# Instance normalisation of 256 MiB on one core: 8 MB tiles in three buffers with one-pass statistics, in place of 4 MB tiles in four buffers with two passes

## The chip, the cores and the metric

One core of one Trainium2 chip. The metric is the device time of one execution in microseconds (us); the profile's "span", from the first to the last instruction, lies some 2 us below it. The kernel before took 1252.11 us (median of 3 runs, 1251.59 to 1254.01).

## The reference

```python
x = np.random.randn(8, 64, 32, 64, 64).astype(np.float32)      # 512 instances of 131072 values
mean = np.mean(x, axis=(2, 3, 4), keepdims=True)
var = np.var(x, axis=(2, 3, 4), keepdims=True)
out = ((x - mean) / np.sqrt(var + 1e-5)).astype(np.float32)
```

256 MiB are read and 256 MiB written, 536.9 MB in all. This input is already very nearly of mean 0 and variance 1, so a kernel that computes slightly wrong statistics, or none, still agrees with the reference within the tolerance.

## The kernel before

An instance is spread over 16 partitions, so a tile holds 8 instances in 128 partitions x 8192 values (32 KiB a partition, 4 MB). There are 64 tiles and four buffers. All transfers go through the SP queue; the store of tile g-2 is issued after the load of tile g.

```python
data_pool = ctx.enter_context(tc.tile_pool(name="data", bufs=4))
...
def issue_compute(g, x_tiles):
    for k in range(KPG):                                   # KPG = 1
        nc.vector.reduce_sum(out=psums[:, k, 0:1], in_=x_tiles[:, k, :], axis=X)
        nc.scalar.activation(out=sq_scratch, in_=x_tiles[:, k, :], func=Square,
                             accum_out=psums[:, k, 1:2])
    nc.tensor.matmul(out=tot, lhsT=ones_t, rhs=psums, start=True, stop=True)
    ...                                                    # mean, variance, scale, bias: 128x1 each
    # normalise in place: VectorE 1/8, ScalarE 1/8, GpSimd 3/4 of the columns
...
LAG = 2
for g in range(n_groups):                                  # 64
    x_tiles = issue_load(g)                                # waits for the buffer's old store
    issue_compute(g, x_tiles)
    pending[g] = x_tiles
    if g >= LAG:
        issue_store(g - LAG, pending.pop(g - LAG))
for g in range(n_groups - LAG, n_groups):
    issue_store(g, pending.pop(g))
```

## Time and profile before

| | before |
|---|---|
| time, span | 1252.11, 1249.7 us |
| bytes moved | 536.9 MB, 430 GB/s over the span |
| DMA engines busy | 99.7% of 16 engines' span |
| VectorE, ScalarE, GpSimd busy | 53%, 44%, 30% |

The first lines are from the page of the kernel before: engines, then the 40 equal slices of the span (DMA: busy tenths of the 16 DMA engines; GB/s: what they moved), the one DMA queue, and groups of instructions (busy us, mean ns of one, idle time before).

```profile
span 1249.7 us, 1827 instructions
...
PE 35.7 (3%) x128; PEld 32.1 (3%) x128; DVE 659.2 (53%) x449; ACT 550.6 (44%) x258; POOL 380.3 (30%) x70
...
DMA  9999999999999999999999999999999999999998
GB/s 403 417 434 434 427 433 430 432 435 430 429 432 434 432 435 429 434 433 434 434 431 433 431 434 434 435 430 432 434 433 436 429 433 434 433 434 435 429 433 357
...
q1 hardware_dynamic: 18432, 536.88, 99.7%
...
L92 DVE TENSOR_REDUCE psums<-x_tiles 128x1 f32<-128x8192 f32 x64 | 555.9, 8686 | 492.9 <-DMA x_tiles<-in_x_dram 492.9
L100 ACT ACTIVATE sq_scratch<-x_tiles 128x8192 bf16<-128x8192 f32 x64 | 449.9, 7029 | 461.3 <-DMA x_tiles<-in_x_dram 461.3
L169 POOL TENSOR_SCALAR x_tiles<-x_tiles,scale,bias 128x6144 f32<-128x6144 f32 x64 | 379.4, 5929 | 855.4 <-DVE bias L149 634.4
L161 ACT ACTIVATE x_tiles<-x_tiles,bias,scale 128x1024 f32<-128x1024 f32 x64 | 79.4, 1241 | 40.5 <-DVE bias L149 40.5
```

The DMA engines are the limit: 9 tenths everywhere but in the last slice, and no other engine above 53%.

The table by stretches of the kernel before. The columns are the window, its length, busy times of the engines with counts, the clock, the DMA share and, last, GB/s:

```profile
core 0: us, PE busy (x) PEld busy (x) DVE busy (x) ACT busy (x) POOL busy (x), PEclk, DMA share, GB/s
300.00:1100.00 800.00, 22.88 (x82) 20.54 (x82) 423.46 (x290) 352.46 (x165) 247.68 (x42) 1.00 1.00 433
80.00:126.00 46.00, 1.67 (x6) 1.50 (x6) 23.97 (x21) 18.83 (x12) 13.88 (x3) 1.00 1.00 432
1230.00:1238.00 8.00, 0.00 (x0) 0.00 (x0) 1.13 (x3) 1.29 (x2) 5.93 (x1) 1.00 0.66 287
1238.00:1249.70 11.70, 0.00 (x0) 0.00 (x0) 0.00 (x0) 0.00 (x0) 0.00 (x0) 1.00 0.75 322
```

In the long middle stretch the engines move 433 GB/s. From 1230 to 1238 us they move 287: the last store waits there for the last tile's computation.

What the SP queue waited for in the kernel before (us in total, times, longest):

```profile
SPq L85 <- DMA out_dram<-x_tiles: 700.8, 60, 12.6
SPq L180 <- POOL x_tiles L169: 303.9, 64, 4.8
```

It mostly waits to issue a load (line 85) until an old store has freed the buffer. One turn of the loop in its timeline (start us, us, engine, line, operation):

```profile
600.16 8.69 DVE L92 TENSOR_REDUCE psums<-x_tiles 128x1 f32<-128x8192 f32 x1 [7.89 <-DMA x_tiles<-in_x_dram]
...
609.83 0.33 SPq L85 DMA_DIRECT2D x_tiles<-in_x_dram  x1
...
611.08 5.93 POOL L169 TENSOR_SCALAR x_tiles<-x_tiles,scale,bias 128x6144 f32<-128x6144 f32 x1 [13.48 <-DVE bias L149]
617.04 0.34 SPq L180 DMA_DIRECT2D out_dram<-x_tiles  x1
619.47 8.69 DVE L92 TENSOR_REDUCE psums<-x_tiles 128x1 f32<-128x8192 f32 x1 [7.79 <-DMA x_tiles<-in_x_dram]
```

When the store is issued at 617.04, three more transfers are unfinished (they were issued at 590.5, 597.6 and 609.8). The queue is deep, though the store's own tile was ready only just before.

### The profile page before, as it was taken

To read this page: it belongs to the slowest core of one execution; us is meant where nothing else is said; L and a number is where in the kernel's file an instruction comes from. 1 tells how busy PE (TensorE), PEld (TensorE's weight loads), DVE (VectorE), ACT (ScalarE), POOL (GpSimd) and SP (SyncE) were. 2 spreads that over 40 slices of the span, in tenths; PEclk is the share of its full clock that TensorE was granted. 3 is DMA by queue.
4 is the path that set the end of the run, shared out by engine and by line. 5 is a ranking of instruction groups with operands and counts; after the bars stand their busy time and mean duration, and the time that the engine had idled before them with its cause. 6 is when DMAs were issued, how large, how long until landed. Compare 5 with 4: busy or idle time off the path is not lost.

```text
span 1249.7 us, 1827 instructions
## 1 busy us (share of the span) xinstructions
PE 35.7 (3%) x128; PEld 32.1 (3%) x128; DVE 659.2 (53%) x449; ACT 550.6 (44%) x258; POOL 380.3 (30%) x70
## 2 busy tenths in 40 slices
PE   0000000000000000000000000000000000000000
PEld 0000000000000000000000000000000000000000
DVE  5736455464554645546546455464554645646543
ACT  5535445354453544535435344354453544534432
POOL 2332332313323233232331322313323233132231
DMA  9999999999999999999999999999999999999998
GB/s 403 417 434 434 427 433 430 432 435 430 429 432 434 432 435 429 434 433 434 434 431 433 431 434 434 435 430 432 434 433 436 429 433 434 433 434 435 429 433 357
DMA packets 18444, 536.99 MB, mean 430 GB/s; under 512 B 2048, under 2 KB 2048, under 8 KB 2048
## 3 DMA queue, kind: packets, MB, share of 16 engines
q1 hardware_dynamic: 18432, 536.88, 99.7%
q14 instruction: 11, 0.09, 0.0%
q8 instruction: 1, 0.02, 0.0%
HBM read 268.44 MB, written 268.44 MB: 430 GB/s over the span
## 4 chain that ended last, share of the span: by engine, by line
DMA 74%; issue 16%; POOL 7%; DVE 1%; POOLq 1%; PE 0%; ACT 0%
DMA out_dram<-x_tiles 39%; DMA x_tiles<-in_x_dram 35%; POOL x_tiles L169 7%; DVE psums L92 1%; POOLq L221 0%; DVE x_tiles L169 0%; POOLq L169 0%; PE tot L108 0%; ACT std L141 0%; DVE scale L147 0%; DVE msq L128 0%; DVE me L117 0%; DVE bias L149 0%; DVE var_eps L131 0%
## 5 line engine op out<-in xcount | busy, mean ns | idle before, releaser
L92 DVE TENSOR_REDUCE psums<-x_tiles 128x1 f32<-128x8192 f32 x64 | 555.9, 8686 | 492.9 <-DMA x_tiles<-in_x_dram 492.9
L100 ACT ACTIVATE sq_scratch<-x_tiles 128x8192 bf16<-128x8192 f32 x64 | 449.9, 7029 | 461.3 <-DMA x_tiles<-in_x_dram 461.3
L169 POOL TENSOR_SCALAR x_tiles<-x_tiles,scale,bias 128x6144 f32<-128x6144 f32 x64 | 379.4, 5929 | 855.4 <-DVE bias L149 634.4
L161 ACT ACTIVATE x_tiles<-x_tiles,bias,scale 128x1024 f32<-128x1024 f32 x64 | 79.4, 1241 | 40.5 <-DVE bias L149 40.5
L141 ACT ACTIVATE std<-var_eps 128x1 f32<-128x1 f32 x64 | 13.0, 203 | 178.7 <-DVE var_eps L131 178.7
L108 PE MATMUL tot<-psums,ones_t 128*128 128x2 f32 x128 | 35.7, 348 | 1193.5 <-DVE psums L92 1193.5
L108 PEld LDWEIGHTS tot<-psums,ones_t 128*128 128x128 f32 x128 | 32.1, 311 | 1197.1 <-issue 1197.1
L169 DVE TENSOR_SCALAR x_tiles<-x_tiles,scale,bias 128x1024 f32<-128x1024 f32 x64 | 52.1, 813 | 2.5
L117 DVE TENSOR_SCALAR me<-tot 128x2 f32<-128x2 f32 x64 | 10.2, 160 | 47.5 <-PE tot L108 47.5
L147 DVE RECIPROCAL scale<-std 128x1 f32<-128x1 f32 x64 | 10.5, 164 | 21.8 <-ACT std L141 21.8
L100 ACT ACTIVATION_READ_ACCUMULATOR sq_scratch<-x_tiles 128x1 f32 x64 | 11.9, 187 | 0.0
L128 DVE TENSOR_TENSOR msq<-me 128x1 f32<-128x1 f32 x64 | 10.2, 159 | 2.2
L131 DVE SCALAR_TENSOR_TENSOR var_eps<-me,msq 128x1 f32<-128x1 f32 x64 | 10.2, 159 | 2.2
L149 DVE SCALAR_TENSOR_TENSOR bias<-me,scale 128x1 f32<-128x1 f32 x64 | 10.2, 159 | 2.2
L100 ACT ACT_TABLE_LOAD x1 | 1.3, 1283 | 0.8 <-PEq L207 0.8
L141 ACT ACT_TABLE_LOAD x1 | 1.3, 1283 | 0.0
L51 DVE MEMSET ones_t<- 128x128 f32 x1 | 0.2, 165 | 0.9 <-PEq L207 0.9
L53 POOL TENSOR_SCALAR_AFFINE_SELECT ones_t<-ones_t 128x128 f32<-128x128 f32 x1 | 0.3, 343 | 0.6 <-DVE ones_t L51 0.6
L62 POOL TENSOR_SCALAR_AFFINE_SELECT ones_t<-ones_t 128x128 f32<-128x128 f32 x1 | 0.3, 338 | 0.1
L207 POOL MEMSET const-float32-0.0<- 128x1 f32 x1 | 0.1, 98 | 0.3 <-issue 0.3
L207 POOL MEMSET const-bfloat16-1.0<- 128x1 bf16 x1 | 0.1, 101 | 0.0
L207 POOL MEMSET const-uint8-127<- 128x1 uint8 x1 | 0.1, 101 | 0.0
(1 smaller groups left out, 0.1 us busy)
## 6 DMA issues: line engine op xcount, KB each, us to landing
x_tiles<-in_x_dram SPq DMA_DIRECT2D x64, 4096.0 KB, 29.0
out_dram<-x_tiles SPq DMA_DIRECT2D x64, 4096.0 KB, 31.5
```

Source lines behind the costliest of these rows:

```text
L92: nc.vector.reduce_sum(out=psums[:, k, 0:1], in_=x_tiles[:, k, :], axis=mybir.AxisListType.X,)
L100: nc.scalar.activation(out=sq_scratch, in_=x_tiles[:, k, :], func=mybir.ActivationFunctionType.Square, accum_out=psums[:, k, 1:2],)
L108: nc.tensor.matmul(out=tot, lhsT=ones_t, rhs=psums, start=True, stop=True,)
L117: nc.vector.tensor_scalar(out=me2, in0=tot, scalar1=inv_F, scalar2=None, op0=mybir.AluOpType.mult,)
L128: nc.vector.tensor_mul(out=msq, in0=mean, in1=mean)
L131: nc.vector.scalar_tensor_tensor(out=var_eps, in0=e2, scalar=eps_f, in1=msq, op0=mybir.AluOpType.add, op1=mybir.AluOpType.subtract,)
L141: nc.scalar.activation(out=std, in_=var_eps, func=mybir.ActivationFunctionType.Sqrt,)
L147: nc.vector.reciprocal(out=scale, in_=std)
L149: nc.vector.scalar_tensor_tensor(out=bias, in0=mean, scalar=-1.0, in1=scale, op0=mybir.AluOpType.mult, op1=mybir.AluOpType.mult,)
L161: nc.scalar.activation(out=x_tiles[:, k, lo:hi], in_=x_tiles[:, k, lo:hi], func=mybir.ActivationFunctionType.Identity, scale=scale[:, k : ...
L169: eng.tensor_scalar(out=x_tiles[:, k, lo:hi], in0=x_tiles[:, k, lo:hi], scalar1=scale[:, k : k + 1], scalar2=bias[:, k : k + 1], op0=mybir ...
L207: nc = _bacc.Bacc("TRN2", target_bir_lowering=False, num_devices=1)
```

## The change

The intent: fewer and larger transfers (rows of 64 KiB), one pass over the data for the statistics in place of two, no GpSimd work, and a last tile in three pieces so that little is left to do after the last load.

```diff
-    SPLIT = 16 ... G = 8 ... LAG = 2
+    SLOTS = 3
+    COLS = 16384                         # a tile: 16 instances, 64 KiB a partition, 8 MB
+    groups = [(i, BIG) for i in range(0, n_inst - BIG, BIG)]          # 31 tiles of 16 instances
+    groups += [... BIG // 2 ..., ... BIG // 4 ..., ... BIG // 4 ...]  # the last: 8, 4 and 4
...
-            nc.vector.reduce_sum(...); nc.scalar.activation(... Square, accum_out=...)
+        for c in range(n_chunks):        # 32 for a whole tile
+            nc.vector.bn_stats(out=st[:, c, :], in_=t[:, c * FMAX : (c + 1) * FMAX])   # 512 columns
+        nc.vector.bn_aggr(out=mv, in_=st[:, 0:n_chunks, :])
...      # mean by one small matmul, variance by a second one
-        # normalise: VectorE 1/8, ScalarE 1/8, GpSimd 3/4
+        cut = t.shape[1] * 3 // 4        # ScalarE [:cut], VectorE [cut:]
...
+    for g in range(n_big):               # 31
+        if g >= SLOTS:
+            store(tiles[g - 2], *groups[g - 2])
+        load(whole(g), *groups[g])
+        if g == SLOTS - 1:
+            store(tiles[0], *groups[0])
+        compute(tiles[g], groups[g][1])
...      # store 29, the three loads of the last tile, store 30, then compute and store each piece
```

With three buffers the queue runs load g-2, store g-3, load g-1, store g-2, load g and so on: store g-2 must be queued before load g-1 has drained.

More of the change, by code (lines that the diff above doesn't have):

```diff
@@ L4 @@
 import concourse.tile as tile
-from concourse import bass_utils, mybir
+from concourse import mybir
 from concourse._compat import with_exitstack
@@ L18 @@
     fp32 = mybir.dt.float32
+    Alu = mybir.AluOpType
+    Act = mybir.ActivationFunctionType
     P = 128
@@ L25 @@
     eps_f = float(eps)
-    SPLIT = 16
-    IPT = P // SPLIT
-    F = n_elem // SPLIT
-    G = 8
-    KPG = G // IPT
-    n_groups = n_inst // G
-    LAG = 2
-    x_packed = x.rearrange("b c d h w -> (b c) (d h w)").rearrange(
-        "(k i) (s f) -> k (i s) f", i=IPT, s=SPLIT
-    )
-    out_packed = out.rearrange("b c d h w -> (b c) (d h w)").rearrange(
-        "(k i) (s f) -> k (i s) f", i=IPT, s=SPLIT
-    )
-    singles = ctx.enter_context(tc.tile_pool(name="singles", bufs=1))
-    data_pool = ctx.enter_context(tc.tile_pool(name="data", bufs=4))
@@ L46 @@
-    scratch_pool = ctx.enter_context(tc.tile_pool(name="scratch", bufs=2))
-    stat_pool = ctx.enter_context(tc.tile_pool(name="stats", bufs=4))
-    psum_pool = ctx.enter_context(tc.tile_pool(name="psum", bufs=4, space=bass.MemoryType.PSUM))
-    ones_t = singles.tile([P, P], fp32)
-    nc.vector.memset(ones_t, 1.0 / SPLIT)
-    blk_pattern = [[-SPLIT, P // SPLIT], [0, SPLIT]]
-    nc.gpsimd.affine_select(
-        out=ones_t,
-        in_=ones_t,
-        pattern=blk_pattern,
-        compare_op=mybir.AluOpType.is_ge,
-        fill=0.0,
-        base=0,
-        channel_multiplier=1,
-    )
@@ L62 @@
-    nc.gpsimd.affine_select(
-        out=ones_t,
-        in_=ones_t,
-        pattern=[[SPLIT, P // SPLIT], [0, SPLIT]],
-        compare_op=mybir.AluOpType.is_ge,
-        fill=0.0,
-        base=SPLIT - 1,
-        channel_multiplier=-1,
-    )
-    inv_F = 1.0 / F
-    c1 = F // 8
-    c2 = F // 4
-    norm_splits = [
-        (nc.vector, 0, c1),
-        (nc.scalar, c1, c2),
-        (nc.gpsimd, c2, F),
-    ]
-    def issue_load(g):
-        x_tiles = data_pool.tile([P, KPG, F], fp32, name="x_tiles")
-        src = x_packed[g * KPG : (g + 1) * KPG].rearrange("k p f -> p k f")
-        nc.sync.dma_start(out=x_tiles, in_=src)
-        return x_tiles
@@ L88, in issue_compute @@
-    def issue_compute(g, x_tiles):
-        psums = stat_pool.tile([P, KPG, 2], fp32, name="psums")
-        for k in range(KPG):
-            nc.vector.reduce_sum(
-                out=psums[:, k, 0:1],
-                in_=x_tiles[:, k, :],
-                axis=mybir.AxisListType.X,
-            )
-            sq_scratch = scratch_pool.tile(
-                [P, F], mybir.dt.bfloat16, name="sq_scratch"
-            )
-            nc.scalar.activation(
-                out=sq_scratch,
-                in_=x_tiles[:, k, :],
-                func=mybir.ActivationFunctionType.Square,
-                accum_out=psums[:, k, 1:2],
-            )
-        tot = psum_pool.tile([P, KPG, 2], fp32, name="tot")
-        nc.tensor.matmul(
-            out=tot,
-            lhsT=ones_t,
-            rhs=psums,
-            start=True,
-            stop=True,
-        )
-        me2 = stat_pool.tile([P, KPG, 2], fp32, name="me2")
-        nc.vector.tensor_scalar(
-            out=me2,
-            in0=tot,
-            scalar1=inv_F,
-            scalar2=None,
-            op0=mybir.AluOpType.mult,
-        )
-        mean = me2[:, :, 0]
-        e2 = me2[:, :, 1]
-        msq = stat_pool.tile([P, KPG], fp32, name="msq")
-        nc.vector.tensor_mul(out=msq, in0=mean, in1=mean)
-        var_eps = stat_pool.tile([P, KPG], fp32, name="var_eps")
-        nc.vector.scalar_tensor_tensor(
-            out=var_eps,
-            in0=e2,
-            scalar=eps_f,
-            in1=msq,
-            op0=mybir.AluOpType.add,
-            op1=mybir.AluOpType.subtract,
-        )
-        std = stat_pool.tile([P, KPG], fp32, name="std")
-        nc.scalar.activation(
-            out=std,
-            in_=var_eps,
-            func=mybir.ActivationFunctionType.Sqrt,
-        )
-        scale = stat_pool.tile([P, KPG], fp32, name="scale")
@@ new lines @@
+    SLOTS = 3
+    FMAX = nc.vector.BN_STATS_FMAX
+    COLS = 16384
+    x_f = x.rearrange("b c d h w -> (b c) (d h w)")
+    out_f = out.rearrange("b c d h w -> (b c) (d h w)")
+    BIG = P * COLS // n_elem
+    groups = [(i, BIG) for i in range(0, n_inst - BIG, BIG)]
+    groups += [
+        (n_inst - BIG, BIG // 2),
+        (n_inst - BIG // 2, BIG // 4),
+        (n_inst - BIG // 4, BIG // 4),
+    ]
+    n_big = n_inst // BIG - 1
+    singles = ctx.enter_context(tc.tile_pool(name="singles", bufs=1))
@@ new lines, with averaging @@
+    data_pool = ctx.enter_context(tc.tile_pool(name="data", bufs=SLOTS))
+    stat_pool = ctx.enter_context(tc.tile_pool(name="stats", bufs=3))
+    psum_pool = ctx.enter_context(
+        tc.tile_pool(name="psum", bufs=2, space=bass.MemoryType.PSUM)
+    )
+    def averaging(split):
+        avg = singles.tile([P, P], fp32, name=f"avg{split}")
+        nc.vector.memset(avg, 1.0 / split)
+        nc.gpsimd.affine_select(
+            out=avg,
+            in_=avg,
+            pattern=[[-split, P // split], [0, split]],
+            compare_op=Alu.is_ge,
+            fill=0.0,
+            base=0,
+            channel_multiplier=1,
+        )
+        nc.gpsimd.affine_select(
+            out=avg,
+            in_=avg,
+            pattern=[[split, P // split], [0, split]],
+            compare_op=Alu.is_ge,
+            fill=0.0,
+            base=split - 1,
+            channel_multiplier=-1,
+        )
+        return avg
@@ new lines, with rows, load, store @@
+    avgs = {n: averaging(P // n) for n in sorted({n for _, n in groups})}
+    def rows(ap, first, n):
+        return ap[first : first + n].rearrange("i (s f) -> (i s) f", s=P // n)
+    def load(t, first, n):
+        nc.sync.dma_start(out=t, in_=rows(x_f, first, n))
+    def store(t, first, n):
+        nc.sync.dma_start(out=rows(out_f, first, n), in_=t)
+    def statistics(t):
+        n_chunks = t.shape[1] // FMAX
+        st = stat_pool.tile(
+            [P, COLS // FMAX, nc.vector.BN_STATS_DIM], fp32, name="st"
+        )
+        for c in range(n_chunks):
+            nc.vector.bn_stats(out=st[:, c, :], in_=t[:, c * FMAX : (c + 1) * FMAX])
+        mv = stat_pool.tile([P, nc.vector.BN_AGGR_DIM], fp32, name="mv")
+        nc.vector.bn_aggr(out=mv, in_=st[:, 0:n_chunks, :])
+        return mv
@@ new lines, in coefficients @@
+    def coefficients(mv, avg):
+        mean_ps = psum_pool.tile([P, 1], fp32, name="mean_ps")
+        nc.tensor.matmul(out=mean_ps, lhsT=avg, rhs=mv[:, 0:1], start=True, stop=True)
+        dist = stat_pool.tile([P, 1], fp32, name="dist")
+        nc.vector.tensor_sub(out=dist, in0=mv[:, 0:1], in1=mean_ps)
+        part = stat_pool.tile([P, 1], fp32, name="part")
+        nc.vector.scalar_tensor_tensor(
+            out=part,
+            in0=dist,
+            scalar=dist,
+            in1=mv[:, 1:2],
+            op0=Alu.mult,
+            op1=Alu.add,
+        )
+        var_ps = psum_pool.tile([P, 1], fp32, name="var_ps")
+        nc.tensor.matmul(out=var_ps, lhsT=avg, rhs=part, start=True, stop=True)
+        var = stat_pool.tile([P, 1], fp32, name="var")
+        nc.vector.tensor_scalar(
+            out=var, in0=var_ps, scalar1=eps_f, scalar2=None, op0=Alu.add
+        )
+        std = stat_pool.tile([P, 1], fp32, name="std")
+        nc.scalar.activation(out=std, in_=var, func=Act.Sqrt)
+        scale = stat_pool.tile([P, 1], fp32, name="scale")
@@ L147, in issue_compute @@
         nc.vector.reciprocal(out=scale, in_=std)
-        bias = stat_pool.tile([P, KPG], fp32, name="bias")
+        bias = stat_pool.tile([P, 1], fp32, name="bias")
         nc.vector.scalar_tensor_tensor(
             out=bias,
-            in0=mean,
+            in0=mean_ps,
             scalar=-1.0,
             in1=scale,
-            op0=mybir.AluOpType.mult,
-            op1=mybir.AluOpType.mult,
-        )
-        for k in range(KPG):
-            for eng, lo, hi in norm_splits:
-                if eng is nc.scalar:
-                    nc.scalar.activation(
-                        out=x_tiles[:, k, lo:hi],
-                        in_=x_tiles[:, k, lo:hi],
-                        func=mybir.ActivationFunctionType.Identity,
-                        scale=scale[:, k : k + 1],
-                        bias=bias[:, k : k + 1],
-                    )
-                else:
-                    eng.tensor_scalar(
-                        out=x_tiles[:, k, lo:hi],
-                        in0=x_tiles[:, k, lo:hi],
-                        scalar1=scale[:, k : k + 1],
-                        scalar2=bias[:, k : k + 1],
-                        op0=mybir.AluOpType.mult,
-                        op1=mybir.AluOpType.add,
-                    )
@@ L178, in issue_store @@
-    def issue_store(g, x_tiles):
-        dst = out_packed[g * KPG : (g + 1) * KPG].rearrange("k p f -> p k f")
-        nc.sync.dma_start(out=dst, in_=x_tiles)
-    pending = {}
-    for g in range(n_groups):
-        x_tiles = issue_load(g)
-        issue_compute(g, x_tiles)
-        pending[g] = x_tiles
-        if g >= LAG:
-            issue_store(g - LAG, pending.pop(g - LAG))
-    for g in range(n_groups - LAG, n_groups):
-        issue_store(g, pending.pop(g))
+            op0=Alu.mult,
@@ new lines, in coefficients, with normalise @@
+            op1=Alu.mult,
+        )
+        return scale, bias
+    def normalise(t, scale, bias):
+        cut = t.shape[1] * 3 // 4
+        nc.scalar.activation(
+            out=t[:, :cut],
+            in_=t[:, :cut],
+            func=Act.Identity,
+            scale=scale,
+            bias=bias,
+        )
+        nc.vector.tensor_scalar(
+            out=t[:, cut:],
+            in0=t[:, cut:],
+            scalar1=scale,
+            scalar2=bias,
+            op0=Alu.mult,
+            op1=Alu.add,
+        )
@@ new lines, with whole, compute @@
+    tiles = {}
+    def whole(g):
+        tiles[g] = data_pool.tile([P, COLS], fp32, name="xt")
+        return tiles[g]
+    def compute(t, n):
+        normalise(t, *coefficients(statistics(t), avgs[n]))
+    for g in range(n_big):
[5 more added lines that the diff above has]
+        compute(tiles[g], groups[g][1])
+    store(tiles[n_big - 2], *groups[n_big - 2])
@@ L194 @@
+    last = whole(n_big)
+    parts = []
+    at = 0
+    for first, n in groups[n_big:]:
+        width = n * n_elem // P
+        parts.append((last[:, at : at + width], first, n))
+        at += width
+    for t, first, n in parts:
+        load(t, first, n)
+    store(tiles[n_big - 1], *groups[n_big - 1])
+    for t, first, n in parts:
+        compute(t, n)
+        store(t, first, n)
 _INS = ['x', 'eps']
```

## The prediction

> **What bounds it now.** The 16 DMA engines. The page's slices show DMA at 9 tenths in all but the last, and the queue table puts 99.7% of 16 engines' span on the one SP queue, with 537 MB moved. No compute engine is above 53%. The slices settle at 430 to 435 GB/s. In the stage table, a mid-run stretch of 19.37 us (one 4 MB load plus one 4 MB store) moves 435 GB/s, the next 432. The Trainium skill, "DMA: Bandwidth & Descriptors", section "Where 436 GB/s comes from", gives 435.2 GB/s as the fabric ceiling; this trace agrees. At 434 the bytes alone need 1237 us, so of the 1249.7 us span about 13 us can be saved at all. Read from the slices' shortfall (estimate): first slice 2.2 us (start), second 1.2, dips in between about 4, last slice 5.5. The tail is real idling: in the timeline the last load lands at 1219.8, its statistics, coefficients and GpSimd part end at 1236.7, and only then goes the last 4 MB store (stages 1230-1240 and 1240-1249.7: 288 and 328 GB/s).
>
> **What changes.** Bytes, queue and engines of the transfers stay. Half as many, twice as large DMAs: rows of 64 instead of 32 KiB; I expect no rate gain, as 433-435 is reached already. ScalarE's squares (450 us) and GpSimd (380 us) vanish, off the critical path, so worth nothing. VectorE gets 32 statistics instructions of 512 per 8 MB tile. Estimate: the 8192-wide reduce took 8.69 us, 1.04 ns an element plus 0.15; 512 gives 0.68 of which neighbours overlap 0.08 (as reduce and the operation before it do), so 0.60-0.65 each, 20 us a tile. VectorE about 24 us per 38.7 us tile.
>
> **The critical question** is latency per tile, since with three buffers the queue runs ... load g-2, store g-3, load g-1, store g-2: the store must be queued within 38.7 us (two 8 MB transfers) of the load's end. Sum (estimate): landing 1.2, statistics 20, aggregation 0.4, two small matmuls with their chain 2.9 (the old chain with one matmul took 2.2), ScalarE's 12288 elements 10.5 (slope from 1024 in 1.24 and 8192 in 7.03 us), store issue to first byte 1.4: 36.4 us. It fits by about 2 us; no stall in steady state.
>
> **At the start** it does not fit: tiles 0-2 load at once, VectorE makes tile 1's coefficients only after tile 0's share, so store 1 comes at about 83 us while store 0 has drained at about 80: 3 to 4 us idle. **At the end** the pieces pay: with 8 MB of store still queued behind the last loads, all three pieces (4, 2, 2 MB) are ready before the queue drains. Tail idle falls from 5.5 to about 1.5 us.
>
> **Sum:** 1237 (434 GB/s) + 2.2 start + 3.6 early stall + 1.3 last receipt = 1244 span; timed runs lie 2.4 above the span: **1246 us** (0.5% faster). Range 1239 to 1262. Faster by over 2%: 0.01 (1227 us would need more than the 435.2 ceiling). Within 2%: 0.89. Slower by over 2%: 0.10.
>
> **Signs.** Right: DMA 9 throughout, one dip in slice 2 or 3 near 80 us, last slice above 400 GB/s, statistics 0.6-0.7 us each, VectorE about 60% busy, GpSimd near 0, chain of waits mostly DMA. Wrong: stores issued late each tile (the SP queue's waits name ScalarE's normalisation for long, dips everywhere), or steady rate leaving 431-435.
>
> **What would make it wrong.** The 2 us slack: a statistics instruction of 0.75 us instead of 0.62 adds 4 us latency per tile, 2 us over; each excess microsecond costs about 15 us in all (two tiles are in flight, 30 tiles). Fewer transfers might save a little per boundary (at most 3 us).

## The result, and the profile after

The change took 1262.85 us (median of 4 runs, 1261.74 to 1263.06) against 1251.85 us (median of 4) for the kernel before: 0.9% slower by the medians. Ratios in this document are the mean time of one kernel's fast runs over that of the other's of the same rounds, so not quite the ratio of the medians; here 1.0082, interval 1.0067 to 1.0096. The prediction was 1246 us, range 1239 to 1262: the measured time is 0.85 us outside, on the slow side.

The page of the change, the lines that answer to those above:

```profile
span 1260.0 us, 1888 instructions
...
PE 39.8 (3%) x136; PEld 34.0 (3%) x136; DVE 749.7 (59%) x1265; ACT 349.1 (28%) x69; POOL 2.1 (0%) x10
...
DMA  9999999999999999999999999999999999999997
GB/s 402 429 433 402 433 433 431 435 426 435 433 433 426 433 433 433 431 431 431 412 433 429 433 431 431 433 412 429 431 431 433 427 422 437 416 431 433 423 441 341
...
q1 hardware_dynamic: 9792, 536.88, 99.5%
...
L93 DVE BATCH_NORM_STATS2 st<-xt 128x6 f32<-128x512 f32 x1024 | 611.7, 676 | 427.4 <-DMA xt<-in_x_dram 427.4
L136 ACT ACTIVATE xt<-xt,bias,scale 128x12288 f32<-128x12288 f32 (+2 forms) x34 | 340.9, 10025 | 17.1 <-DVE bias L124 17.1
...
L95 DVE BATCH_NORM_AGGREGATE mv<-st 128x2 f32<-128x192 f32 (+2 forms) x34 | 33.0, 969 | 1.1
```

Bytes and busy share are as they were (9 tenths everywhere, 99.5%), but the slices don't hold 433: some show 402, 412, 423, 426. The durations that I had estimated came out well: the statistics take 676 ns each and start 0.59 us apart, 19.1 us a tile (estimated 20), ScalarE's part 10.6 us (10.5); only the aggregation was dearer (1.02 us against 0.4).

The table by stretches of the change, same columns as before:

```profile
300.00:1100.00 800.00, 24.03 (x82) 20.52 (x82) 470.62 (x786) 227.45 (x42) 0.00 (x0) 1.00 1.00 429
80.00:126.00 46.00, 1.17 (x4) 1.00 (x4) 18.52 (x32) 11.96 (x3) 0.00 (x0) 1.00 1.00 412
1210.00:1254.00 44.00, 3.51 (x12) 3.00 (x12) 24.73 (x53) 16.24 (x7) 0.00 (x0) 1.00 1.00 428
1254.00:1260.00 6.00, 0.00 (x0) 0.00 (x0) 0.00 (x0) 0.00 (x0) 0.00 (x0) 1.00 0.11 46
```

The middle runs at 429 GB/s instead of 433, the start's stretch at 412 instead of 432. The tail is full until 1254 us; then a few engines go on for nearly 5 us, at 46 GB/s over the last 6 us.

What the SP queue waits for in the change:

```profile
SPq L85 <- DVE xt L143: 944.5, 34, 45.7
SPq L85 <- ACT xt L136: 262.7, 34, 8.2
...
SPq L82 <- DMA out_dram<-xt: 1.5, 1, 1.5
```

It no longer waits for buffers, but for the tile to be ready (the first two lines): each store is now issued the moment its normalisation ends. The prediction named this as a sign of its being wrong, but the sign proves little: the run with half the statistics (below) shows 905.5 and 258.7 us in the same two lines and loses nothing. One turn of the loop in the change's timeline:

```profile
548.13 0.33 SPq L85 DMA_DIRECT2D out_dram<-xt  x1
548.51 0.42 SPq L82 DMA_DIRECT2D xt<-in_x_dram  x1
553.97 19.08 DVE L93 BATCH_NORM_STATS2 st<-xt 128x6 f32<-128x512 f32 x32 [14.13 <-DMA xt<-in_x_dram]
573.08 1.02 DVE L95 BATCH_NORM_AGGREGATE mv<-st 128x2 f32<-128x192 f32 x1
...
576.75 2.41 DVE L143 TENSOR_SCALAR xt<-xt,scale,bias 128x4096 f32<-128x4096 f32 x1
576.80 10.63 ACT L136 ACTIVATE xt<-xt,bias,scale 128x12288 f32<-128x12288 f32 x1 [0.47 <-DVE bias L124]
587.45 0.33 SPq L85 DMA_DIRECT2D out_dram<-xt  x1
587.84 0.42 SPq L82 DMA_DIRECT2D xt<-in_x_dram  x1
593.18 19.09 DVE L93 BATCH_NORM_STATS2 st<-xt 128x6 f32<-128x512 f32 x32 [14.02 <-DMA xt<-in_x_dram]
```

The load that was issued at 548.51 is the last thing in the queue. The store that follows it comes at 587.45, and the load's landing shows at 593.18, where the statistics of its tile begin. So there seem to be 5.7 us in hand. But a load lands when the *last* of the 16 DMA engines is done. The trace has a record of every packet; of this load the first engine was done at 588.5 us and the last at 592.9. For the first engine the store came 1 us ahead, not 5.7. (A few engines make this gap: from 600 to 900 us the twelfth engine ends a transfer 0.55 us after the first, the last one 3.9 us after it, in the median.)

### Where the time is, from the packet records

Most packets of one size take the same time: 1.213 us for 32 KiB, 2.418 us for 64 KiB. I call what a packet takes beyond this its *slow time*, and divide sums by 16 to get us of the span. *Ahead* is the time from a store's issue to the first engine's end of the load queued before it (median of 300 to 1100 us). *Spread* is the time between the first and the last engine's end of one transfer (median, same stretch). None of the views above prints these; they are worked out from the packet records, the landings and the issue times. The smaller rows of the last tile are counted at the rate of the run's main packet size; at their own usual times the slow time of a run is 0.1 to 0.3 us less.

| us of the span | before | change | difference |
|---|---|---|---|
| all packets at their usual time | 1242.1 | 1238.0 | -4.1 |
| semaphore writes | 1.2 | 0.6 | -0.6 |
| slow time of packets | 3.2 | 14.9 | +11.7 |
| idle: fewer than 16 packets in flight (start, holes, end) | 7.2 | 8.7 | +1.5 |
| overlap: more than 16 packets in flight | -4.0 | -2.2 | +1.8 |
| span | 1249.7 | 1260.0 | +10.3 |

(Packet records of one engine overlap by a trifle, so their sum is more than the time they need; the last two rows count the packets in flight at every moment.) The larger rows do save something: 4.1 us in packets and 0.6 in semaphore writes, less 1.8 of overlap, so 2.9 us net. The slow time takes it back four times over. In the turn shown above it lies mostly where the queue turns from the store to the next load: eleven packets that started between 565.9 and 566.5 us, the last of store 549 to 569, took 0.28 to 0.90 us too long each. So it is in the whole middle of the run: of 8.4 us of slow time from 300 to 1100 us, 4.8 lie in the last packets of a store, 1.2 just after the turn to the load, and only 2.1 around the turn from a load to the late store. The load had by then been queued for some 20 us, so the slow packets are mostly not those that wait for a late transfer.

### The profile page after: what moved, and what is told of

Same layout as the page of the kernel before. It is cut to its first block, busy times and chain, and to the rows that moved or that the text cites. A ratio compares the mean times of both kernels' runs of the same rounds, so it can differ in the third digit from the quotient of the medians.

```text
span 1260.0 us, 1888 instructions
## 1 busy us (share of the span) xinstructions
PE 39.8 (3%) x136; PEld 34.0 (3%) x136; DVE 749.7 (59%) x1265; ACT 349.1 (28%) x69; POOL 2.1 (0%) x10
## 3 DMA queue, kind: packets, MB, share of 16 engines
q1 hardware_dynamic: 9792, 536.88, 99.5%
## 4 chain that ended last, share of the span: by engine, by line
DMA 56%; DVE 27%; ACT 13%; PE 2%; issue 1%; SPq 0%; ACTq 0%
DMA xt<-in_x_dram 53%; DVE st L93 24%; ACT xt L136 13%; DMA out_dram<-xt 2%; DVE mv L95 1%; PE var_ps L114 1%; PE mean_ps L101 1%; SPq L85 0%; DVE part L105 0%; ACT std L120 0%; DVE var L116 0%; DVE dist L103 0%; DVE scale L122 0%; DVE bias L124 0%; DVE xt L143 0%
## 5 line engine op out<-in xcount | busy, mean ns | idle before, releaser
L93 DVE BATCH_NORM_STATS2 st<-xt 128x6 f32<-128x512 f32 x1024 | 611.7, 676 | 427.4 <-DMA xt<-in_x_dram 427.4
L136 ACT ACTIVATE xt<-xt,bias,scale 128x12288 f32<-128x12288 f32 (+2 forms) x34 | 340.9, 10025 | 17.1 <-DVE bias L124 17.1
L120 ACT ACTIVATE std<-var 128x1 f32<-128x1 f32 x34 | 6.9, 203 | 872.2 <-DVE var L116 872.2
L143 DVE TENSOR_SCALAR xt<-xt,scale,bias 128x4096 f32<-128x4096 f32 (+2 forms) x34 | 77.8, 2287 | 1.2
L101 PE MATMUL mean_ps<-mv,avg 128*128 128x1 f32 x68 | 19.9, 362 | 1177.4 <-DVE mv L95 1177.4
L101 PEld LDWEIGHTS mean_ps<-mv,avg 128*128 128x128 f32 x68 | 17.0, 311 | 1180.2 <-DVE mv L95 1137.3
L95 DVE BATCH_NORM_AGGREGATE mv<-st 128x2 f32<-128x192 f32 (+2 forms) x34 | 33.0, 969 | 1.1
L114 PE MATMUL var_ps<-part,avg 128*128 128x1 f32 x68 | 19.9, 362 | 18.0 <-DVE part L105 18.0
L114 PEld LDWEIGHTS var_ps<-part,avg 128*128 128x128 f32 x68 | 17.0, 310 | 20.9 <-DVE part L105 20.9
L105 DVE SCALAR_TENSOR_TENSOR part<-dist,mv 128x1 f32<-128x1 f32 x34 | 7.4, 218 | 1.1
```

What stands on the lines that cost most here:

```text
L93: nc.vector.bn_stats(out=st[:, c, :], in_=t[:, c * FMAX : (c + 1) * FMAX])
L95: nc.vector.bn_aggr(out=mv, in_=st[:, 0:n_chunks, :])
L101: nc.tensor.matmul(out=mean_ps, lhsT=avg, rhs=mv[:, 0:1], start=True, stop=True)
L105: nc.vector.scalar_tensor_tensor(out=part, in0=dist, scalar=dist, in1=mv[:, 1:2], op0=Alu.mult, op1=Alu.add,)
L114: nc.tensor.matmul(out=var_ps, lhsT=avg, rhs=part, start=True, stop=True)
L120: nc.scalar.activation(out=std, in_=var, func=Act.Sqrt)
```

## The experiments

Two theories to start with. **Late store**: the store is queued so late that the first engines find next to nothing queued when they finish a load; that makes packets slow. **Large transfer**: rows of 64 KiB, or 8 MB transfers, are slower where the queue turns, whenever the store comes. All kernels are the change with the stated edit unless said otherwise. Every run was also measured beside the kernel before, whose medians were 1251.0 to 1252.0 us.

### Half the tile on ScalarE (stores 3.5 us sooner)

```diff
-        cut = t.shape[1] * 3 // 4
+        cut = t.shape[1] // 2
```

> The change with one number altered: ScalarE normalises half of each tile instead of three quarters (10.6 us becomes about 7.0), VectorE the other half (2.4 becomes 4.6), so each store can be queued about 3.5 us sooner after its load. Theory 'late store' (the engines that finish a load first find no store queued; the stores are queued only about 1 us before the first engine's end of load, this keeps the engines in step, and in step each turn from store to load costs): the spread of the engines grows freely, the slow last packets go away, 1250 to 1256 us. Rival 'large transfer' (64 KiB rows or 8 MB transfers are themselves slower at each turn): no change but the start's stall of about 1 us, 1260 to 1263 us.

1260.45 us (ratio to before 1.0068): inside the rival's range, outside that of the late store. Slow time 12.8 us instead of 14.9. The packet records say why it helped so little: the spread grew with the room, from 3.9 to 7.1 us, until the stores were again only 1.5 us ahead of the first engine (1.35 in the change). Giving 3.5 us gave the spread 3.2.

### 15/16 of the tile on ScalarE (stores 2.6 us later)

```diff
-        cut = t.shape[1] * 3 // 4
+        cut = t.shape[1] * 15 // 16
```

> The opposite dose: ScalarE normalises 15/16 of each tile (about 13.2 us instead of 10.6), so each store is queued about 2.6 us later. Theory 'late store': the slack that is left, about 1 us before the first engine and 4 to 5 us before the last, is used up; between 15 and 40 us slower than the change, 1275 to 1303 us. Rival 'large transfer': the mean of the engines still has a store queued in time, under 5 us slower, 1262 to 1268 us.

1267.41 us (1.0124). Some 5 us slower than the change: inside the rival's range by the time, and well short of my 15 to 40. The slow time rose to 20.4 us (ahead 0.8), as the late store says; but the engines closed up, the spread fell to 2.1 us, and the last engine was done 1.5 us after the median one instead of 4.4. So part of the lateness was paid with spread. The prediction's rule "15 us for each excess microsecond" is refuted.

### Transfers in two halves, statistics backwards: a control that failed

```diff
+    # load and store: two DMAs, columns [0:8192] and [8192:16384]
-            for c in range(n_chunks):
+            for c in reversed(range(n_chunks)):
```

> The change with each 8 MB transfer issued as two of 4 MB (column halves, rows of 32 KiB), nothing else; the statistics run from the last half backwards, so they can't begin before the whole tile is there and the store is as late as in the change. Theory 'late store': as slow as the change, 1259 to 1266 us. Rival 'large transfer': back to the kernel before's packet behaviour, 1248 to 1255 us.

1258.82 us (1.0055). This run can't tell the theories apart. The backward order was to keep the store late, but in the trace the first 16 statistics of a tile wait for the first half's load only and start 9.7 us before the second half lands; the store was as early as in the next run. By itself it shows less slow time (4.4 us).

### Transfers in two halves, statistics forwards

```diff
+    # load and store: two DMAs, columns [0:8192] and [8192:16384]
```

> As the run with halves and backward statistics, but the statistics run forwards, so they begin when the first half has landed and each store can be queued about 9 us sooner. Same transfers, same sizes, same order. Theory 'late store': 1246 to 1254 us, stores queued about 10 us ahead. Rival 'large transfer': the same time as the backward run, within 3 us.

1257.56 us (1.0047), 3.6 us slower than the late store theory allowed, and within 3 us of the backward run, as the rival had it; but the two runs turned out to be equally early, so this doesn't speak for the rival. The slow time did go (4.3 us, ahead 5.8), and the middle ran at 432 GB/s. But half the engines were done by 1247.5 us and all except one by 1250, and this one worked until 1255.0. That is a second cost that I come back to.

### The transfers alone, rows of 64 KiB

```diff
     def compute(t, n):
-        normalise(t, *coefficients(statistics(t), avgs[n]))
+        return                            # output wrong on purpose: a copy of x
```

> The change with all computation taken out (output wrong on purpose): the same 8 MB transfers with rows of 64 KiB in the same order and three buffers, each store waiting only for its load. Measures the transfers alone, with the queue always full. Theory 'rows of 64 KiB turn slowly': slow last packets remain, 1250 to 1258 us. Rival 'late store': with nothing late the slow packets go, 1243 to 1248 us.

1250.15 us (0.9985). The time lies at the edge of the range for 'rows of 64 KiB turn slowly' (1250 to 1258), but the slow time is 4.8 us: 64 KiB rows are not slow of themselves. My number for the late store (1243 to 1248) was too low because the engines end between 1241.0 and 1247.0 us. My prediction of 1246 us for the whole kernel lies below what its transfers take with no computation at all.

### The transfers alone, rows of 32 KiB

```diff
+    # whole tiles: "(k i) (s f) -> k (i s) f" with k=2, s=16, as [p k f]: two rows of 32 KiB a partition
     def compute(t, n):
+        return                            # output wrong on purpose
```

> The same without computation (output wrong on purpose) and the same 8 MB transfers, but in rows of 32 KiB (16 a DMA engine instead of 8). If the row size is what matters: less slow-packet time than with rows of 64 KiB by some 8 us, each packet's own rate 0.3% lower. If the 8 MB transfer or the order matters: the same slow packets as with rows of 64 KiB.

1255.9 us (1.0034), slow time 5.0 us, as with 64 KiB. The profiled runs of the two differ by 4.2 us: net of overlap the packets take 2.3 us more (0.2%), and idling is 1.6 us more, with a wider spread at the end (1242.8 to 1251.2 us).

### Stores on ScalarE's queue

```diff
     def store(t, first, n):
-        nc.sync.dma_start(out=rows(out_f, first, n), in_=t)
+        nc.scalar.dma_start(out=rows(out_f, first, n), in_=t)
```

> The change with its stores issued by ScalarE's queue instead of the SP queue, nothing else. Every DMA engine then has loads and stores to choose from and never turns as a whole from one to the other. Theory 'turns cost': the slow last packets go, 1244 to 1252 us. Rival 'late store': a late store leaves the load to fill in, but the total is as before, 1256 to 1264 us.

1380.96 us (1.103): both theories missed by far. From its page (slices and queues):

```profile
DMA  9999899998999999989999899998999999999949
GB/s 426 409 378 399 365 426 395 380 409 367 426 395 365 422 369 395 424 367 403 388 395 426 367 393 376 391 419 367 394 391 399 416 375 393 367 399 422 383 195 395
...
q1 hardware_dynamic: 4896, 268.44, 49.0%
q10 hardware_dynamic: 4896, 268.44, 44.9%
```

With loads and stores side by side a load of 8 MB takes 35.1 us from issue to landing in the median; in the change it takes some 19.6 once the store before it is done. The rate swings between 365 and 426 GB/s. The loads' packets took 41.3 ns a KiB in the mean against 37.8 for the stores', so the slow time did not go: it is 57 us. Idling, counted as in the table above, is 86 us (8.7 in the change). That three buffers no longer cover the longer loads would explain the idling; this run alone does not show it.

### The kernel before with its hole filled

```diff
-    LAG = 2
+    LAG = 3
-    data_pool = ... bufs=4
+    data_pool = ... bufs=5
```

> The kernel before with five buffers and stores three tiles behind instead of two, so that 12 MB of stores are queued behind the last load and the idle hole before the last store is filled; nothing of the change else. My prediction's reading (the hole costs about 4 us): 1246 to 1249 us. Theory 'straggler' (some DMA engines run up to 5.8 us behind the others and are never idle in the hole; filled or not, the last one ends at the same time): within 1.5 us of the kernel before.

1252.4 us (1.0006, interval 0.9993 to 1.002): nothing gained. Its tail, by stretches (columns as above):

```profile
1230.00:1242.00 12.00, 0.00 (x0) 0.00 (x0) 0.00 (x0) 0.00 (x0) 0.00 (x0) 1.00 1.01 434
1242.00:1250.00 8.00, 0.00 (x0) 0.00 (x0) 0.00 (x0) 0.00 (x0) 0.00 (x0) 1.00 0.25 107
```

The stretch from 1230 to 1242 us, 287 GB/s before for 8 us of it, is now at 434: the hole is filled. But the engines don't end together. The median one is done at 1243.5 us, the last at 1248.9; in the kernel before these are 1247.4 and 1248.5. In the kernel before, the last store was issued at 1236.7 us, and the three engines that lag landed their parts of the store before it at 1238.9 to 1239.2: they never waited in the hole. It let the others wait for them.

### Late, with rows of 32 KiB

```diff
+    # whole tiles as [p k f] with k=2 (two rows of 32 KiB a partition, 8 MB a transfer);
+    # computation as in the change, so the values are slightly wrong on purpose
```

> The change's instructions and its lateness, in 8 MB transfers with rows of 32 KiB: a tile holds two sets of eight instances side by side, while the statistics are still made as for one set (values wrong on purpose, work the same). Theory 'late store': slow packets as in the change (some 11 to 15 us in all; the change has 15), and 0.3% slower packets on top: 1261 to 1268 us. Rival 'rows of 64 KiB turn slowly when late': slow packets of some 4 to 6 us, 1252 to 1258 us.

1267.97 us (1.0129), slow time 18.3 us, ahead 1.2. Its middle stretch, columns as above:

```profile
300.00:1100.00 800.00, 24.66 (x84) 21.07 (x84) 472.96 (x789) 224.64 (x42) 0.00 (x0) 1.00 1.00 427
```

The rows are those of the kernel before, the lateness that of the change, and the slow time is there. "Rows of 64 KiB turn slowly" is refuted: 32 KiB rows are as slow when they are as late.

### Early, with rows of 64 KiB

```diff
-        n_chunks = t.shape[1] // FMAX
+        n_chunks = t.shape[1] // FMAX // 2      # statistics of half the columns, wrong on purpose
```

> The change with statistics from the first half of each tile's columns only (values wrong on purpose), so each store can be queued about 9.5 us sooner; transfers and their order untouched, rows of 64 KiB. Theory 'late store': slow packets fall from 15 to about 5 us, and the start's stall goes: 1249 to 1254 us. Rival (lateness doesn't matter; the engines' computation slows the packets, which the run without computation lacked): 1258 to 1263 us.

1252.17 us (1.0005). Slow time 4.1 us, ahead 8.3. Its table by stretches:

```profile
300.00:1100.00 800.00, 23.50 (x80) 20.08 (x80) 275.03 (x471) 218.68 (x41) 0.00 (x0) 1.00 1.00 433
1242.00:1250.50 8.50, 0.00 (x0) 0.00 (x0) 0.00 (x0) 0.00 (x0) 0.00 (x0) 1.00 0.14 58
```

The same transfers in the same order as in the change, with ScalarE's, VectorE's and TensorE's other work running beside them, move 433 GB/s instead of 429 in the middle. VectorE has 275 us of work there instead of 471, so a rival is left, that less work and not the earlier store helped; the correct kernel with early stores, below, has 424 us on VectorE and more on ScalarE than the change (304 us against 227), and its slow time goes as well. Together with the run before, these two decide for the late store. The last line shows the other cost again: 58 GB/s in the last 8.5 us.

### Loads in halves, stores whole

```diff
+    # load: two DMAs, columns [0:8192] and [8192:16384]; store: one DMA
```

> A correct kernel made from what was found: loads in two column halves (rows of 32 KiB), so the statistics begin with the first half and each store is about 9 us earlier; stores whole, rows of 64 KiB. Theory 'late store': slow packets about 5 us, packets at the mean of both rates: 1250 to 1256 us, at best level with the kernel before.

1256.79 us (1.0042), just above the range. Slow time 3.8 us (each packet against the usual time of its own size), as low as in the other early runs; the last engine is done at 1253.6 us, 7.5 us after the median one.

### A correct kernel with early stores

```diff
+        # ScalarE sums the last quarter of the columns, VectorE has the other three
+        for k, func in enumerate((Act.Identity, Act.Square)):
+            nc.scalar.activation(out=junk[:, : w - q], in_=t[:, q:], func=func,
+                                 accum_out=sums[:, k : k + 1])
         for c in range(n_chunks):               # 24 instead of 32
...      # both sums into one [P, 2] right-hand side: one matmul instead of two
-        cut = t.shape[1] * 3 // 4
+        cut = t.shape[1] // 2
```

> A correct kernel with the change's transfers, order and rows of 64 KiB, its stores made about 8 to 9 us earlier by dividing the work: ScalarE sums the last quarter of each tile (sum and sum of squares) while VectorE makes the statistics of the rest, one matmul instead of two, and normalisation is halved between the two engines. Theory 'late store': slow packets of 4 to 6 us as in the run with half the statistics, 1250 to 1255 us, level with the kernel before and about 10 us better than the change. Rival (it was the wrong-on-purpose run's smaller VectorE load and not its earlier stores that helped): 1258 to 1263 us.

1255.56 us (1.0032), half a us above the range, 7 us better than the change, not level with the kernel before. Slow time 4.5 us, and the middle as it should be:

```profile
300.00:1100.00 800.00, 11.74 (x40) 10.01 (x40) 423.71 (x686) 304.22 (x122) 0.00 (x0) 1.00 1.00 433
1242.00:1253.90 11.90, 0.00 (x0) 0.00 (x0) 0.00 (x0) 0.00 (x0) 0.00 (x0) 1.00 0.11 45
```

What is left over stands in the second line. The median engine is done at 1242.7 us and all except one by 1244.3; that one is done at 1252.4. Without it this kernel would have a span of about 1246 us, an estimate from the last but one engine plus the 1.5 us from the last engine's end to the end of the span.

### Work taken off one engine: two runs that answer nothing

```diff
-    store(tiles[n_big - 1], *groups[n_big - 1])
+    # the same store as partitions [0:120] and [120:128]
```

> The repaired kernel, with the last whole store (8 MB) issued as 120 partitions, then 8 partitions. By the Trainium skill, page 'DMA: Bandwidth & Descriptors', on how the number of engines is chosen, the first runs on the 15 lowest-numbered engines and the second on the 8 lowest, so engine 15 gets 19 us less and engines 0 to 7 get 2.4 us more. If the straggler is always engine 15: about 7 us better than the repaired kernel, 1246 to 1250 us. If it is among 8 to 14: unchanged, 1254 to 1257 us. If it is among 0 to 7: 2 us worse, 1257 to 1260 us. If it varies from run to run: a mixture, with a spread of some us among the runs.

1277.03 us (1.0197), outside all the ranges. The page "DMA: Bandwidth & Descriptors" of the Trainium skill, section on why a DMA increments its semaphore by 16, says that the number of engines is the largest k up to 16 that divides the slowest dimension, 15 for 120 partitions. The packet records agree: exactly 15.0 engines were busy between 1210 and 1218 us. But the stretch moved half the usual rate:

```profile
1206.00:1246.00 40.00, 1.75 (x6) 1.50 (x6) 21.55 (x52) 15.52 (x18) 0.00 (x0) 1.00 1.04 233
```

The cost of such a store, some 20 us, buries the lag that it was to uncover. The second run did the same in the kernel before's form:

> The kernel before with five buffers and stores three tiles behind, with its last store but two (4 MB) issued as 120, then 8 partitions. If the straggler is engine 15: about 3 us better than the same without it, 1248 to 1250 us. If it is among 8 to 14: unchanged, 1251 to 1254 us; among 0 to 7: 1 us worse.

1260.02 us (1.0067), for the same reason. Which engine lags, and whether it is always the same one, stays open.

### Lateness and slow time, run by run

| run | ahead, us | slow time, 300 to 1100 us | spread, us | last engine after the median one, at the end | GB/s, 300 to 1100 us |
|---|---|---|---|---|---|
| stores 2.6 us later | 0.8 | 13.9 | 2.1 | 1.5 | 426 |
| late, rows of 32 KiB | 1.2 | 11.5 | 4.0 | 4.2 | 427 |
| the change | 1.35 | 8.4 | 3.9 | 4.4 | 429 |
| stores 3.5 us sooner | 1.5 | 6.8 | 7.1 | 6.6 | 431 |
| correct, early | 5.3 | 1.3 | 8.1 | 9.8 | 433 |
| halves, forwards | 5.8 | 1.5 | 8.6 | 7.5 | 432 |
| early, half the statistics | 8.3 | 1.0 | 7.0 | 7.1 | 433 |
| kernel before | 15.7 | 0.5 | 5.8 | 1.1 (closed up by its hole) | 433 |
| transfers alone, 64 KiB | 33.2 | 1.8 | 5.1 | 5.3 | 433 |

These are the runs on one queue that keep the whole computation or bear on the argument; the others on this queue lie in line with them (0.5 to 2.6 us of slow time in the same stretch, 6 to 31 us ahead). The slow time follows how far ahead of the *first* engine the store is queued, over two row sizes and with much or little computation. Inside the change's own run it does so too: from 126 to 300 us, while the spread is still 1 to 2 us and the stores 3 to 4 us ahead, the slow time is 0.7 us (0.4 for each 100 us); from 600 to 900 us, with a spread of some 4 us and the stores about 1 us ahead, it is 4.1 us (1.4 for each 100). One rival is left half open. A late store also draws most of the engines together: the median engine ends a transfer 0.3 us after the first one in the change (600 to 900 us), but 0.5 to 1.0 us after it in the kernel before and the early runs; perhaps engines that turn together are slow, and lateness only brings them together. Being together is not enough: from 126 to 300 us the kernel before has its median engine 0.3 us after the first too, with stores about 18 us ahead, and 0.4 us of slow time for each 100 us. But no run holds the engines together with an early store for longer. What goes on inside a DMA engine was not shown either, nor why the slow packets are mostly the last of a store (4.8 of 8.4 us in the change, 9.8 of 13.9 with stores 2.6 us later, 9.6 of 11.5 late with rows of 32 KiB, 0.0 of 0.5 in the kernel before), one transfer after the turn that was late.

## Why the prediction was wrong, point by point

- **The bound** was right. DMA is at 9 tenths before and after.
- **ScalarE's and GpSimd's work being worth nothing** was right: GpSimd fell from 380 to 2 us and nothing was gained.
- **"No rate gain" from larger rows** was right within the reserve that the text made ("at most 3 us"): 2.9 us were gained, net of overlap.
- **The latency of a tile** was right. From the landing at 553.97 us to the store's issue at 587.45 are 33.5 us; the same terms of the sum (20 + 0.4 + 2.9 + 10.5) make 33.8. The other two terms were too large: 0.3 us from the last packet to the start of the statistics (estimated 1.2), and about 0.9 from a store's issue to its first packet (estimated 1.4; in the kernel before, the last store is issued at 1236.7 us and its first packets start at about 1237.55).
- **"It fits by about 2 us; no stall in steady state"** is the step that failed. The latency was held against 38.7 us as if the 16 engines were one. But the computation starts when the last engine lands its part, and the queue must not run dry for the first, 3.9 us earlier in the median. With the terms as measured there were 4 us in hand for the last engine (38.7 less 34.7); the spread took all of them. By the issue times the store came 1.35 us ahead of the first engine's end. It was paid not as a stall, which the DMA row would show, but as slow packets inside a row of 9s: 10.8 us after the first 126 us where the prediction had none (the kernel before has 1.2 there). The Trainium skill says it on the page "DMA: Bandwidth & Descriptors", section on why a DMA increments its semaphore by 16: the engines of a DMA finish independently, and only the full count means that all has landed. This trace agrees, with its spread of 3.9 us; I had not carried it into the sum.
- **"Tail idle falls from 5.5 to about 1.5 us"** failed as well. The hole was filled, but 5.2 us of idling at the end remained (5.0 in the kernel before), since the last engine ended 4.4 us after the median one. Filling the hole in the kernel before by itself gained nothing (1.0006). A hole in which the lagging engines still work costs only what the last of them waits.
- **The early stall**, estimated at 3.6 us, was about 0.9 us of idling more than in the kernel before, and the slow time of the first 126 us, 4.1 us, is 2.1 above it. That the two make 3.0 us, near the estimate, is luck: the kind was not as predicted.
- **"Each excess microsecond costs about 15 us"** was wrong: 2.6 us more latency cost some 5 us.
- **The sum.** Predicted span 1244, measured 1260.0. Slow time after the start +10.8, idling at the end +3.9, the start +1.2, small holes in the middle +0.5, the packets themselves -0.6.

So the mechanism feared in "what would make the prediction wrong", late stores, was the one that struck, but with the estimated latencies met: the 38.7 us were the wrong yardstick. The 16 us by which the sum missed are nearly all slow packets and idling at the end.

What stays open: why one engine falls further and further behind when the stores are early (0.5 us of spread at the start, 6 to 10 near the end), which one it is, and why packets before a turn are slow when the store is late. No correct version beat the kernel before: the best correct one reached 1255.56 us. The transfers of the change with no computation reached 1250.15.

## What to carry to other kernels

When you hold a tile's latency against the time that the queue covers, count from the last DMA engine's landing to the first engine's running dry, and take off the spread of the engines, which the landing times show; a few us of slack on paper can be none. A row of 9s for the DMA engines does not prove that they work at full rate: look at GB/s, and at the time of single packets. And before filling a hole at the end, see whether all engines wait in it, because a hole that only lets the fast ones wait for the slow ones is nearly free.

## What the Trainium skill lacked or had wrong

- "DMA: Bandwidth & Descriptors": it says that the engines of a DMA finish independently, but gives no size for it. Here they drift apart over hundreds of us, from 0.5 us to between 2 and 10 us, and one engine can be 9.8 us behind the median at the end.
- The same page has nothing on a queue that is refilled late while it isn't yet empty: with the next store issued about 1 us before the first engine ends its load, packets lost 8 to 14 us in 800, with no idling in the DMA row; from 5 us on, 0.5 to 2.6 us.
- The same page, "Issuing engines are not separate DMA queues", says that issuing from several engines only saves issue time. Moving the stores to ScalarE's queue made this kernel 10% slower (1380.96 us against 1251.92): loads and stores then run side by side, and the section has no warning that this can cost time.
- The same page's rule for how many engines a DMA uses held (15 for 120 partitions), but it gives no warning about the rate: the store of 120 partitions ran at about half (the stretch shown above, 233 against 433 GB/s).
- The same page gives about 27 GiB/s for one DMA engine. A packet of 64 KiB takes 2.418 us here, which is 27.1 GB/s or 25.2 GiB/s, so the number fits as GB/s. One of 32 KiB takes 1.213 us; net of overlap some 5 ns are saved when two rows are one (the two runs without computation).
- The same page's warning box lets the HBM side bind at about 358 GB/s for transfers between HBM and SBUF. With this one core at work 433 GB/s were held over 800 us, loads and stores together, so the ceiling of 435.2 GB/s is the one that fits. The page's note on its own measurements says that 358 is each core's share when two of them stream; the box leaves this out.
- "VectorE: DVE Perf Modes", section on the fixed extra latency of SBUF sources: it gives 58 + N cycles and calls it too low for the duration of one operation, with about 150 as the measured fixed part. Here the two numbers go with different things: a statistics instruction of 512 values lasts 676 ns (137 cycles over 512 at 0.96 GHz), and independent ones start 0.593 us apart, which is (58 + 512) / 0.96 ns. For a row of independent instructions the smaller number is the one to sum.
- No page has the times of the statistics instructions themselves: 676 ns for 512 values, 1.02 us for the aggregation of 32 of them.
